# Weight sums of a seven-product block multiplication, formed in DRAM ahead of time instead of in SBUF on demand

## Chip, cores and metric

The kernel runs on one NeuronCore of a Trainium2 chip. The metric is the device time of one execution in microseconds, lower is better.

## The reference

A decoder trunk of two layers on a sequence of 512 tokens with 1024 features, float32. Layer 0 is a retention with four heads, layer 1 a stick-breaking attention with sixteen; each is followed by a gated feed-forward with a causal depthwise convolution of width 3. What the change touches is the last step of the feed-forward:

```python
def _conv_ffn(h, w_up, conv_w, conv_b, w_down):
    u = h @ w_up                       # 512 x 1024 @ 1024 x 5632
    u = lax.conv_general_dilated(...) + conv_b
    gate, val = jnp.split(u, 2, axis=-1)
    return (jax.nn.silu(gate) * val) @ w_down      # 512 x 2816 @ 2816 x 1024

for i in range(DEPTH):
    x = x + mixer_i(_rmsnorm(x, ...))  # retention, then stick-breaking
    x = x + _conv_ffn(_rmsnorm(x, ...), ...)
return _rmsnorm(x, final_norm)
```

## The kernel before

Activations lie in SBUF with features on the 128 partitions and tokens along the free dimension: eight tiles `x[m]` of 128x512. Every float32 product is made of three matmuls on a high and a low part in the type float32r (`mm3`, L133). Weights come from DRAM as chunks of 128x1024 (512 KB). `chunk` (L117) takes a `raw` buffer (`raw`, L114, three of them), loads it on SyncE's queue (L121), and `parts` (L124) casts it on ScalarE to `hi` (L129) and subtracts on VectorE to `lo` (L130); there are five buffers of `hi` and five of `lo`. A chunk feeds 24 matmuls of 512 columns in the projections. The source order gives a priority, and the framework fixes the order of instructions on each engine and queue when the kernel is built; each engine and each queue then works through its list in order and waits by semaphores.

`retention` (L371) reads x, makes the first four projections (`first4`, L144), forms the norm factor `self.r` by a `rsqrt` and then walks over four heads: `ret_qk`, `ret_v`, `ret_scores`, `ret_av`, `ret_y`, `out_proj`. `ret_v` uses four chunks together for 96 matmuls (`token_major`, L283).

`ffn` (L511) loops over the 22 blocks f of 128 hidden features: two up-projections, convolution, activation (`ffn_act`, L410). The down-projection goes in stages of blocks (`STAGES`). Layer 0 has stages of 8, 8 and 6 blocks, layer 1 of 8, 6 and 4, and then a tail of 4. The first two stages of each layer (`FAST`) are done by `fast_down` (L455), one call for each half of the output features, and start once the next two blocks are up-projected. Tokens are split in two halves, blocks in pairs, output features in quarters, and the 2x2 block product is made of seven products instead of eight. Each product multiplies a quarter-size weight, or a sum of such weights, by one of the operands that `ffn_act` prepared (`X11`, `T1`, `T2`, `T3`, `T4`, `X21`, `X22`). The weights are w11, w12, w21, w22 and the four sums

```
s1 = w21 + w22      s2 = s1 + w11      s3 = w11 + w21      s4 = s2 + w12
```

`quarter` (L445) issues the matmuls (L452) of one product for one of two PSUM banks; a product is 12 matmuls of 256 columns in each of two banks where the stage has 8 blocks, 9 where it has 6. After a product, `add` (L477) adds or subtracts the PSUM contents so far to the tiles `x[m]` on VectorE (L480). The products X11, T2, T3 and T4 accumulate in the banks `x`, T1 and X22 in `z`, X21 alone in two `acc` banks.

Before the change the sums are made in SBUF: a tile `sums` (two buffers) is loaded with w21 by SyncE (L471), w22 is added by a DMA that accumulates, issued by GpSimd (L469), the tile is split into hi and lo for T1, then w11 is accumulated onto it for T2, and later w12 for X22; a `raw` tile gets w11 and later w21 for T3. The products stand in the order T1, X11, T2, X21, T3, X22, T4.

Of the kernel before, what the change touches and what calls it, by code (L numbers as in the profile page):

```python
# [9 lines left out]
F32 = mybir.dt.float32  # L10
F32R = mybir.dt.float32r
AF = mybir.ActivationFunctionType
ALU = mybir.AluOpType
AX = mybir.AxisListType

P = 128
# [10 lines left out]
CH = 1024  # L27
STAGES = (((0, 8), (8, 16), (16, 22)), ((0, 8), (8, 14), (14, 18)))
FAST = (2, 2)
# [7 lines left out]
class Kernel:  # L37
# [12 lines left out]
    def __init__(self, ctx, tc, t):  # L50
        self.tc, self.nc, self.t = tc, tc.nc, t
        self.const = ctx.enter_context(tc.tile_pool(name="const", bufs=1))
        self.wp = ctx.enter_context(tc.tile_pool(name="wp", bufs=1))
        self.ap = ctx.enter_context(tc.tile_pool(name="ap", bufs=1))
        self.ps = ctx.enter_context(tc.tile_pool(name="ps", bufs=1, space=bass.MemoryType.PSUM))
        self.n = 0
        self.pp = None
        self.att_pool()
        self.phase("mix")
# [52 lines left out]
        return hi, lo  # L112

    def raw(self):  # L114
        return self.wp.tile([P, CH], F32, tag="raw", bufs=3, name=self.name("raw"))

    def chunk(self, c, cols=CH):  # L117

        nc = self.nc
        raw = self.raw()  # L120
        nc.sync.dma_start(raw[:, :cols], c)  # L121
        return self.parts(raw, cols)

    def parts(self, raw, cols=CH):  # L124
        nc = self.nc
        hi = self.wp.tile([P, CH], F32R, tag="hi", bufs=5, name=self.name("hi"))
        lo = self.wp.tile([P, CH], F32R, tag="lo", bufs=5, name=self.name("lo"))
        raw, hi, lo = raw[:, :cols], hi[:, :cols], lo[:, :cols]
        nc.scalar.copy(hi, raw)  # L129
        nc.vector.tensor_sub(lo, raw, hi.bitcast(F32))  # L130
        return hi, lo
# [101 lines left out]
    def setup(self):  # L233
        nc, t = self.nc, self.t
        c = lambda n, cols, dt=F32: self.const.tile([P, cols], dt, name=n)
        self.vec = c("vec", t["vec"].shape[1])
        nc.scalar.dma_start(self.vec[:, : 5 * KD], t["vec"][:, : 5 * KD])
        self.x = [c(f"x{m}", S) for m in range(KD)]
        self.ones = c("ones", P, F32R)
        nc.vector.memset(self.ones.bitcast(F32), 1.0)  # L240
        self.eps = c("eps", 1)
        nc.vector.memset(self.eps, EPS)

        nc.scalar.activation(c("table", 1), self.eps, AF.Sqrt)
        self.diag = c("diag", S)
        nc.vector.memset(self.diag, 0.0)

        warm = self.one()
        for i in range(WARM):
            nc.tensor.matmul(warm[:, :HALF], self.ones.bitcast(F32), self.diag[:, :HALF], start=i == 0, stop=i == WARM - 1)  # L250
        self.ident = self.diag[:, S - P :]
        nc.gpsimd.affine_select(
            out=self.ident, in_=self.ident, compare_op=ALU.not_equal, fill=1.0, base=0,
            pattern=[[-1, P]], channel_multiplier=1,
        )
# [115 lines left out]
    def retention(self):  # L371
        nc, t = self.nc, self.t
        first = self.first4("rfirst", load=True)
        self.cos, self.sin = self.sb("cs", S + P)[:, :S], self.sb("cs", S + P)[:, :S]
        nc.sync.dma_start(self.cos, t["cos"])
        nc.sync.dma_start(self.sin, t["sin"])
        nc.sync.dma_start(self.vec[:, 5 * KD :], t["vec"][:, 5 * KD :])
        nc.vector.tensor_mul(self.cos, self.cos, self.r)
        nc.vector.tensor_mul(self.sin, self.sin, self.r)
        self.rc = self.token_major_r()  # L380
        y = None
        for h in range(RH):
            q, k, tail = self.ret_qk(h, first if h == 0 else [])
            v = self.ret_v(h)
            if 0 < h < RH - 1:
                self.out_proj("rout", 4 * (h - 1), y, None)
            p = self.ret_scores(h, q, k, tail)
            o = self.ret_av(h, v, p)
            last, y = y, self.ret_y(h, o)
        self.out_proj("rout", 4 * (RH - 2), last, None)  # L390
        self.out_proj("rout", 4 * (RH - 1), y, 1)
# [63 lines left out]
    def fast_down(self, l, s, ops, half):  # L455


        nc, t = self.nc, self.t[f"fast{l}_{s}"][half]
        cols = 2 * len(ops) * P
        w11, w12, w21, w22 = t[0], t[1], t[2], t[3]  # L460
        first, second = slice(0, Q), slice(Q, S)
        x = [self.psum("x", 2) for _ in range(2)]
        z = [self.psum("z", 2) for _ in range(2)]
        sums = self.wp.tile([P, CH], F32, tag="sums", bufs=2, name=self.name("sums"))
        raw = self.raw()

        def load(to, w, add=False):
            if add:
                nc.gpsimd.dma_start(to[:, :cols], w, accum_op=ALU.add)  # L469
            else:  # L470
                nc.sync.dma_start(to[:, :cols], w)  # L471

        def product(to, w, n, start=False):
            for p in range(2):
                self.quarter(to[p], w, p, ops, n, start)

        def add(row, tokens, of, sign=1):  # L477
            for p in range(2):
                x = self.x[4 * half + 2 * p + row][:, tokens]
                (nc.vector.tensor_add if sign > 0 else nc.vector.tensor_sub)(x, x, of[p][:, :Q])  # L480

        load(sums, w21)
        load(sums, w22, True)
        load(raw, w11)
        w = self.parts(sums, cols)
        product(z, w, self.T1, True)
        add(1, second, z, -1)
        load(sums, w11, True)
        w = self.parts(raw, cols)
        product(x, w, self.X11, True)  # L490
        add(0, first, x)
        load(raw, w21, True)
        w = self.parts(sums, cols)
        product(x, w, self.T2)
        add(0, second, x)
        load(sums, w12, True)
        w = self.chunk(w12, cols)
        y = [self.acc() for _ in range(2)]
        product(y, w, self.X21, True)
        add(0, first, y)  # L500
        w = self.parts(raw, cols)
        product(x, w, self.T3)
        add(1, second, x, -1)
        w = self.parts(sums, cols)
        product(z, w, self.X22)
        add(0, second, z)
        w = self.chunk(w22, cols)
        product(x, w, self.T4)
        add(1, first, x, -1)

    def ffn(self, l, last):  # L511
        a, s = [], 0
        first = self.first4(f"ufirst{l}")
        self.phase("ffn")
        for f in range(NF):
            a.append(self.ffn_act(l, f, first[2 * f : 2 * f + 2] if f < 2 else (None, None)))
            if f == 1:
                self.swap_pool()
            if s < 2 and f == STAGES[l][s][1] + 1:
                lo, hi = STAGES[l][s]  # L520
                for half in range(2):
                    self.fast_down(l, s, a[lo + 1 : hi : 2], half)
                s += 1
        self.swap_pool()
        self.down(l, a, s, last)
        self.phase("mix" if last is not None else None)
        return a
# [310 lines left out]
```

## Time and profile before

| | |
|---|---|
| median of 3 runs | 1402.52 us (1402.23 to 1402.61) |
| the profiled execution | 1401.99 us, span 1400.2 us |
| TensorE busy | 1371.3 us, 98% of the span |
| VectorE busy | 1012.9 us, 72% |
| ScalarE busy | 618.4 us, 44% |
| mean granted TensorE clock | 0.994 |
| moved by DMA | 142.69 MB, 102 GB/s over the span |

The profile is of one execution. The span runs from its first to its last instruction; the execution's own time is 1.8 us longer. Engines are named PE (TensorE), PEld (its weight loads), DVE (VectorE), ACT (ScalarE), POOL (GpSimd) and SP (SyncE); a q behind the name is the engine's queue of DMA issues or its sequencer. L129 is line 129 of the kernel. Busy TensorE time is the union of its matmuls, whose records overlap, so the pace is read from the distance of their starts. A granted clock of 1.00 is 2.4 GHz, a lower mean says that part of the stretch ran at 1.2 GHz.

### The profile page before, as it was taken

What the parts mean: (1) busy time and instruction counts of PE and PEld (TensorE: products, weight loads), DVE (VectorE), ACT (ScalarE), POOL (GpSimd) and SP (SyncE); (2) the same over time, 40 slices, a digit from 0 to 9 for tenths busy, and PEclk for the clock granted to TensorE, in tenths of its full rate; (3) what the DMA queues carried; (4) which work ended last, traced back from release to release, by engine and by line L of the source; (5) the groups of instructions that cost most, each with busy time, mean ns of one, the idle gap of its engine ahead of it and who ended that gap; (6) DMA issues with size and microseconds to landing.
All of it is one profiled execution on the core that took longest, in us unless ns stands there. A gap on an engine that the chain in (4) does not pass through costs nothing.

```text
span 1400.2 us, 18420 instructions
## 1 busy us (share of the span) xinstructions
PE 1371.3 (98%) x7208; PEld 1163.2 (83%) x7208; DVE 1012.9 (72%) x1416; ACT 618.4 (44%) x876; POOL 34.8 (2%) x101
## 2 busy tenths in 40 slices
PE   9999999999999998999999999999999998998997
PEld 7888888888888888889888888787788897897887
DVE  7764564655669885777667788989799875776765
ACT  6433332434355442444344654654265443343434
POOL 0000000000000000001000000000000010010000
PEclk9999999999999999999999999999999999999999
DMA  8433133222233357336622422111133365245231
GB/s 288 122 94 103 55 107 104 62 90 73 78 91 120 105 108 184 103 96 135 177 77 65 134 84 62 61 54 39 45 108 119 95 127 170 84 87 162 62 89 61
DMA packets 45638, 142.69 MB, mean 102 GB/s; under 512 B 5104, under 2 KB 7280, under 8 KB 45552
## 3 DMA queue, kind: packets, MB, share of 16 engines
q1 hardware_dynamic: 39424, 124.45, 28.8%
q0 software_dynamic: 4608, 15.73, 6.8%
q10 hardware_dynamic: 1520, 1.33, 0.3%
q8 instruction: 57, 0.93, 0.3%
q14 instruction: 29, 0.24, 0.1%
HBM read 139.40 MB, written 2.10 MB: 101 GB/s over the span
## 4 chain that ended last, share of the span: by engine, by line
PE 84%; issue 7%; DVE 4%; DMA 3%; ACT 1%; POOL 0%; DVEq 0%; ACTq 0%; POOLq 0%
PE acc L136 21%; PE acc L138 21%; PE acc L137 21%; PE x L452 4%; PE att L136 3%; PE att L137 3%; PE att L138 3%; DMA sums<-in_fast 3%; PE z L452 2%; PE one L608 2%; PE z L582 1%; PE tp L600 1%; PE acc L452 1%; DVE lo L130 1%; ACT hi L129 1%
## 5 line engine op out<-in xcount | busy, mean ns | idle before, releaser
L129 ACT CAST hi<-raw 128x1024 fp32r<-128x1024 f32 (+2 forms) x253 | 244.3, 967 | 395.6 <-PE acc L137 257.9
L137 PE MATMUL acc<-xl,hi 128*128 128x512 f32 x960 | 374.6, 390 | 0.0
L136 PE MATMUL acc<-xh,hi 128*128 128x512 f32 x960 | 374.2, 390 | 0.0
L138 PE MATMUL acc<-xh,lo 128*128 128x512 f32 x960 | 374.2, 390 | 0.0
L130 DVE TENSOR_TENSOR lo<-raw,hi 128x1024 fp32r<-128x1024 f32 (+2 forms) x253 | 281.5, 1114 | 49.6 <-ACT hi L129 48.0
L138 PEld LDWEIGHTS acc<-xh,lo 128*128 128x128 f32 x960 | 180.2, 188 | 37.9 <-issue 0.5
L136 PEld LDWEIGHTS acc<-xh,hi 128*128 128x128 f32 x960 | 180.2, 188 | 36.9 <-issue 0.5
L137 PEld LDWEIGHTS acc<-xl,hi 128*128 128x128 f32 x960 | 180.3, 188 | 35.8
L404 DVE SCALAR_TENSOR_TENSOR tt<-tt,vec,tt 128x511 f32<-128x511 f32 (+1 forms) x176 | 131.1, 747 | 4.3 <-ACT tt L402 1.7
L401 DVE TENSOR_TENSOR tt<-acc,rr 128x512 f32<-128x512 f32 x80 | 55.1, 688 | 73.3 <-PE acc L138 73.3
L138 PE MATMUL acc<-hi,xl 128*128 128x512 f32 (+1 forms) x256 | 86.0, 336 | 0.0
L137 PE MATMUL acc<-lo,xh 128*128 128x512 f32 (+1 forms) x256 | 85.9, 336 | 0.0
L136 PE MATMUL acc<-hi,xh 128*128 128x512 f32 (+1 forms) x256 | 85.9, 336 | 0.0
L188 DVE TENSOR_TENSOR x<-x,acc 128x512 f32<-128x512 f32 x72 | 48.9, 685 | 50.6 <-PE acc L138 50.4
L452 PE MATMUL x<-oh,hi 128*128 128x256 f32 x240 | 70.4, 293 | 14.3 <-DVE x L480 14.3
L402 ACT ACTIVATE tt<-tt,vec 128x512 f32<-128x512 f32 x88 | 71.4, 812 | 10.1 <-DVE tt L401 9.0
L136 PE MATMUL acc<-yy,hi 128*128 128x512 f32 x192 | 75.1, 391 | 0.0
L138 PE MATMUL acc<-yy,lo 128*128 128x512 f32 x192 | 75.1, 391 | 0.0
L137 PE MATMUL acc<-yy,hi 128*128 128x512 f32 x192 | 75.0, 391 | 0.0
L452 PE MATMUL x<-ol,hi 128*128 128x256 f32 x240 | 69.8, 291 | 0.0
L452 PE MATMUL x<-oh,lo 128*128 128x256 f32 x240 | 69.7, 290 | 0.0
L452 PEld LDWEIGHTS x<-oh,hi 128*128 128x128 f32 x240 | 48.1, 200 | 15.0 <-ACT hi L129 9.7
(173 smaller groups left out, 2297.4 us busy)
## 6 DMA issues: line engine op xcount, KB each, us to landing
raw<-in_up SPq DMA_DIRECT2D x80, 512.0 KB, 3.7
sums<-in_fast POOLq DMA_DIRECT2D x18, 512.0 KB, 5.5
raw<-in_fast SPq DMA_DIRECT2D x18, 512.0 KB, 3.6
raw<-in_rv SPq DMA_DIRECT2D x16, 512.0 KB, 3.6
raw<-in_rg SPq DMA_DIRECT2D x16, 512.0 KB, 4.1
raw<-in_rout SPq DMA_DIRECT2D x16, 512.0 KB, 3.6
raw<-in_rqk SPq DMA_DIRECT2D x12, 512.0 KB, 3.6
raw<-in_sqk SPq DMA_DIRECT2D x12, 512.0 KB, 3.7
```

What stands on the lines that cost most here:

```text
L129: nc.scalar.copy(hi, raw)
L130: nc.vector.tensor_sub(lo, raw, hi.bitcast(F32))
L136: mm(out, a[0], b[0], start=start, stop=False)
L137: mm(out, a[0], b[1], start=False, stop=False)
L138: mm(out, a[1], b[0], start=False, stop=stop)
L188: self.nc.vector.tensor_add(self.x[m], self.x[m], ps)
L401: nc.vector.tensor_mul(u, ps, self.r)
L402: nc.scalar.activation(c, u, AF.Identity, scale=w[2], bias=w[3])
L404: nc.vector.scalar_tensor_tensor(c[:, i:], u[:, : S - i], w[2 - i], c[:, i:], op0=ALU.mult, op1=ALU.add)
L452: mm(out[:, :Q], a[ai], b[bi], start=start and k + i == 0, stop=k == nk - 1 and i == 2, skip_group_check=not start)
L582: nc.tensor.matmul(z[:, :nz], q[:, i * P : (i + 1) * P], k[:, :nz], start=m == 0, stop=m == 1)
L608: self.nc.tensor.matmul(o[e * DH : (e + 1) * DH, i * P : (i + 1) * P], v[p // 4 * NT + j][:, h * DH : (h + 1) * DH], aT[e][:, j * P : (j + ...
```

## The change

The four sums of each half of each fast stage are made once, in DRAM tiles, by transfers that GpSimd issues, during the retention (`weight_sums`, called after the first `rsqrt`, gated by a copy on GpSimd of one column of `self.r`). For each stage and half these are four plain copies and four accumulating transfers: w21 to s1, w11 to s3, then w22 onto s1, w21 onto s3; s1 to s2, w11 onto s2; s2 to s4, w12 onto s4. `fast_down` then loads each of its seven weights with `chunk`, as the projections do, in the order X11, T1, T2, X21, T3, X22, T4. The tiles `sums` are gone, and `raw` has five buffers instead of three. The matmuls, the adds to x and the arithmetic of a sum stay.

```diff
     def raw(self):
-        return self.wp.tile([P, CH], F32, tag="raw", bufs=3, name=self.name("raw"))
+        return self.wp.tile([P, CH], F32, tag="raw", bufs=5, name=self.name("raw"))
...
+        self.dp = ctx.enter_context(tc.tile_pool(name="dp", bufs=1, space=bass.MemoryType.DRAM))
...
+        self.gate = c("gate", 1)
...
         self.rc = self.token_major_r()
+        self.weight_sums()
...
-        w11, w12, w21, w22 = t[0], t[1], t[2], t[3]
+        w11, w12, w22 = t[0], t[1], t[3]
+        s1, s2, s3, s4 = (d[half] for d in self.sums[l, s])
...
-        sums = self.wp.tile([P, CH], F32, tag="sums", bufs=2, name=self.name("sums"))
-        raw = self.raw()
-
-        def load(to, w, add=False):
-            if add:
-                nc.gpsimd.dma_start(to[:, :cols], w, accum_op=ALU.add)
-            else:
-                nc.sync.dma_start(to[:, :cols], w)
...
         def product(to, w, n, start=False):
+            w = self.chunk(w, cols)
             for p in range(2):
                 self.quarter(to[p], w, p, ops, n, start)
...
-        load(sums, w21)
-        load(sums, w22, True)
-        load(raw, w11)
-        w = self.parts(sums, cols)
-        product(z, w, self.T1, True)
+        product(x, w11, self.X11, True)
+        add(0, first, x)
+        product(z, s1, self.T1, True)
         add(1, second, z, -1)
-        load(sums, w11, True)
-        w = self.parts(raw, cols)
-        product(x, w, self.X11, True)
-        add(0, first, x)
-        load(raw, w21, True)
-        w = self.parts(sums, cols)
-        product(x, w, self.T2)
+        product(x, s2, self.T2)
         add(0, second, x)
-        load(sums, w12, True)
-        w = self.chunk(w12, cols)
         y = [self.acc() for _ in range(2)]
-        product(y, w, self.X21, True)
+        product(y, w12, self.X21, True)
         add(0, first, y)
-        w = self.parts(raw, cols)
-        product(x, w, self.T3)
+        product(x, s3, self.T3)
         add(1, second, x, -1)
-        w = self.parts(sums, cols)
-        product(z, w, self.X22)
+        product(z, s4, self.X22)
         add(0, second, z)
-        w = self.chunk(w22, cols)
-        product(x, w, self.T4)
+        product(x, w22, self.T4)
         add(1, first, x, -1)
+
+    def weight_sums(self):
+        nc, tc, t = self.nc, self.tc, self.t
+        self.sums = {}
+        gate = nc.gpsimd.tensor_copy(self.gate, self.r[:, :1])
+        gate = getattr(gate, "ins", gate)
+        with tc.issue_after(gate):
+            for l in range(2):
+                for s in range(FAST[l]):
+                    cols = t[f"fast{l}_{s}"].shape[3]
+                    v = [[None] * 2 for _ in range(4)]
+                    for half in range(2):
+                        for i in range(4):
+                            d = self.dp.tile([P, cols + 16], F32, tag=f"s{l}{s}{i}{half}", bufs=1, name=self.name("sum"))
+                            v[i][half] = d[:, :cols]
+                    self.sums[l, s] = v
+                    for to, of, add in ((0, 2, 0), (2, 0, 0), (0, 3, 1), (2, 2, 1), (1, None, 0), (1, 0, 1), (3, None, 0), (3, 1, 1)):
+                        for half in range(2):
+                            w = t[f"fast{l}_{s}"][half][of] if of is not None else v[0 if to == 1 else 1][half]
+                            if add:
+                                nc.gpsimd.dma_start(v[to][half], w, accum_op=ALU.add)
+                            else:
+                                nc.gpsimd.dma_start(v[to][half], w)
```

## Rows read from the trace of the kernel before

**Rows 1.** The page, part 1: busy time, share of the span, instructions.

```profile
PE 1371.3 (98%) x7208; PEld 1163.2 (83%) x7208; DVE 1012.9 (72%) x1416; ACT 618.4 (44%) x876; POOL 34.8 (2%) x101
```

**Rows 2.** Stretches: us, busy PE, PEld, DVE, ACT, POOL; clock, DMA share, GB/s.

```profile
512.02:558.78 46.76, 42.05 (x338) 41.87 (x336) 32.01 (x49) 16.78 (x16) 4.36 (x5) 0.96 0.68 169
645.84:691.00 45.16, 42.22 (x338) 41.87 (x337) 29.76 (x46) 15.88 (x16) 4.43 (x6) 0.96 0.68 174
1130.60:1177.00 46.40, 41.77 (x338) 41.59 (x337) 32.10 (x49) 16.77 (x16) 4.36 (x5) 0.96 0.64 159
1242.30:1278.45 36.15, 31.96 (x253) 31.75 (x252) 25.82 (x45) 13.66 (x16) 2.62 (x3) 0.95 0.51 129
...
15.00:20.00 5.00, 5.00 (x23) 4.14 (x23) 4.47 (x8) 3.02 (x6) 0.00 (x0) 1.00 1.03 368
...
35.00:40.00 5.00, 5.00 (x24) 4.14 (x23) 5.00 (x9) 2.11 (x5) 1.53 (x2) 1.00 0.87 170
...
30.00:486.00 456.00, 455.50 (x2075) 379.19 (x2074) 296.78 (x388) 184.44 (x247) 1.88 (x2) 1.00 0.32 95
...
512.00:534.00 22.00, 22.00 (x185) 21.97 (x184) 17.14 (x27) 9.55 (x9) 2.62 (x3) 1.00 0.66 144
...
544.00:562.00 18.00, 18.00 (x131) 17.44 (x131) 10.11 (x16) 5.25 (x5) 0.86 (x1) 0.94 0.69 198
```

**Rows 3.** Timeline of TensorE: first matmul of the first stage, first after it.

```profile
512.02 0.28 PE L452 MATMUL z<-oh,hi 128*128 128x256 f32 x1
...
558.78 0.40 PE L136 MATMUL acc<-xh,hi 128*128 128x512 f32 x1
```

**Rows 4.** Chain of waits in the first fast stage (start, us, what).

```profile
534.33 5.60 DMA sums<-in_fast
540.03 1.05 ACT hi L129
...
542.80 4.61 PE x L452 x24
547.42 2.88 PE acc L452 x24
```

**Rows 5.** Waits of TensorE and the SP queue (total us, times, longest).

```profile
PE x L452 <- DVE x L480: 14.3, 4, 4.7
...
PE att L136 <- ACT pp L327: 0.4, 1, 0.4
...
SPq L121 <- DVE lo L130: 991.8, 206, 22.7
```

**Rows 6.** The page, parts 3 and 6: DMA queues, and issues to landing.

```profile
q1 hardware_dynamic: 39424, 124.45, 28.8%
q0 software_dynamic: 4608, 15.73, 6.8%
...
sums<-in_fast POOLq DMA_DIRECT2D x18, 512.0 KB, 5.5
raw<-in_fast SPq DMA_DIRECT2D x18, 512.0 KB, 3.6
```

**Rows 7.** Timeline of VectorE near the end of the first fast stage.

```profile
549.56 0.41 DVE L480 TENSOR_TENSOR x<-x,acc 128x256 f32<-128x256 f32 x1
...
551.29 1.23 DVE L130 TENSOR_TENSOR lo<-raw,hi 128x1024 fp32r<-128x1024 f32 x1 [0.54 <-ACT hi L129]
```

**Rows 8.** Landing times: loads before 30 us, and the tile sums.

```profile
raw<-in_rv SPq DMA_DIRECT2D x4, 512.0 KB, 5.4
...
DMA to landing us min/median/max: 2.7/5.4/8.5
```

**Rows 9.** The chain of waits in the first head.

```profile
48.76 3.91 DMA raw<-in_rqk
...
53.80 0.52 ACT pp L327
...
55.10 0.23 PE acc L136
```

## The prediction, made blind

> **What bounds the kernel now.** I read the page first: TensorE is busy 1371.3 of 1400.2 us [rows 1], so only 28.9 us of its idle time can be won, plus whatever it lost at a low clock. The busy share cannot say where these are, so the next view was the table by stretch, with one stretch for each of the four `fast_down` stages (two in each layer) [rows 2]; their ends are the first matmul of the stage and the first of another line after it [rows 3]. TensorE is idle there for 46.76 - 42.05 = 4.71, 2.94, 4.63 and 4.19 us, together 16.47. The granted clock of the same rows is 0.95 to 0.96, so part of each stage ran at 1.2 GHz instead of 2.4.
>
> The chain of waits shows the cause in the first stage [rows 4]. In its second half the chain goes through a transfer `sums<-in_fast` (5.60 us to landing) and the ScalarE cast of that tile, and only then do 24 matmuls start, which take 4.61 us where the next 24 take 2.88: the low clock comes behind the pause. TensorE's wait is listed as one on VectorE's add to x [rows 5]; by the chain the add only stood behind the late split of `sums` in VectorE's queue. The transfer is the accumulating one that makes w21+w22+w11 of w21+w22 in place: it can't start before the earlier product's split has read the tile, and the next product's weights can't be cast before it lands. Two `sums` buffers hide this in a first half (no idle time from 512 to 534 [rows 2]), not in a second.
>
> A matmul of 256 columns takes 2.88/24 = 0.12 us at full clock [rows 4]. A stage of 8 blocks has 14 products of 24, 40.32 us; the one of 6 blocks 14 of 18, 30.24 us. The stages take 46.76, 45.16, 46.40 and 36.15 us [rows 2]. The differences, 6.44, 4.84, 6.08 and 5.91, sum to **23.27 us**: 16.47 idle and 6.80 of slow clock. The other idle time, 28.9 - 16.47 = 12.4 us, lies outside these stages and is not touched.
>
> **The change, part by part.**
>
> *Removed: the accumulating transfers on the path.* After it every product's weights are a plain chunk: load, cast, subtract, as in the up-projection. No chunk depends on another, so loads and casts run ahead as far as five raw and five hi/lo buffers allow. A plain 512 KB load of `in_fast` lands in 3.6 us against 5.5 for an accumulating one [rows 6]. Whether chunks can feed a product every 2.88 us I read from the end of the first stage, where the remaining products of before were already cast ahead or plain: the 24 matmuls from 547.42 on take their 2.88 us [rows 4]. There VectorE needs 1.23 us for a subtraction and 0.41 for each of two adds, 2.05 us a product [rows 7], and ScalarE 1.05 [rows 4], both under 2.88. Over a whole stage VectorE's 32.01 us (25.82 in the last) stand against 40.32 (30.24) [rows 2]. Loads: 512 KB each 2.88 us is 182 GB/s; 198 GB/s moved between 544 and 562 with a DMA share of 0.69 [rows 2], accumulating transfers included. So I take the whole 23.27 us as won; the lower bound is 16.47 less a restart at low clock, should a small pause remain.
>
> *Moved: the order of the products.* X11 now comes first and T1 second. X11, then T2 into the same `x` banks becomes X11, T1, T2, which puts 2.88 us between the product and its successor in the bank. In exchange the last product of the first half (T4, into x) is followed directly by X11 of the second half. One bank has 1.44 us from its own end to its next matmul, as the other bank's 12 matmuls lie between. In the steady stretch the add of the first bank (at 549.56, done 549.97) ended 0.33 us before the other bank's matmuls did, at 547.42 + 2.88 = 550.30 [rows 4, 7]. So 0 as the value; if a subtraction of 1.23 us stands one place worse, 1.23 - 0.33 = 0.9 us at each of four boundaries, 3.6 us as the upper bound. I put 0.4 us.
>
> *Moved and added: 64 transfers on GpSimd's queue after the first `rsqrt`.* Each half of a stage makes four plain copies and four accumulates, all with a DRAM destination: 32 + 32 transfers of 512 KB (384 KB in the last stage), 15.73 MB plain and 15.73 MB accumulating. GpSimd's queue is blocked while they wait for each other; what is behind them in that queue are the small memsets of the attention, which follows the first feed-forward. Engine time: the queue of accumulating transfers used 6.8% of 1400.2 us for 15.73 MB, 6.05 us for each MB, and the plain queue 28.8% for 124.45 MB, 3.24 us [rows 6]. That gives 51 + 95 = 146 us if DRAM to DRAM costs what DRAM to SBUF does; I know no row for a DRAM destination, so doubled, 292 us, is the other end. The stretch from 30 to 486 has a share of 0.32, or 146 us [rows 2]; it would rise to 0.64, or 0.96 at the high end. Below one either way, and the sums of layer 0's first stage, a quarter of it, are wanted only shortly before 512 us [rows 3].
>
> What the loads feel: between 15 and 20 us the share was 1.03 and TensorE stayed busy [rows 2]; loads then landed in 5.4 us instead of 3.6 [rows 8]. The sensitive place is the burst of casts after `ret_v`, where four chunks come free together: there ScalarE waits for `raw<-in_rqk` (3.91 us) in front of the cast `pp` that TensorE needs [rows 9], and TensorE lost 0.4 us [rows 5]. If such a load took the 8.5 us that the slowest transfer of `sums` took [rows 8], about 5 us at each of four heads, 20 us, would be the upper bound. Against it stand five raw buffers instead of three: four loads may be complete before the burst, and the queue of loads waited mostly for a buffer (991.8 us on `lo`) [rows 5], not for data. The lower bound is -0.5, all idle time of TensorE between 30 and 486 [rows 2]. I take +1.5 us, nearer to the low end, as the only such wait in the trace cost 0.4.
>
> The Trainium skill (DMA: Bandwidth & Descriptors, Issuing engines are not separate DMA queues) says that transfers from GpSimd and SyncE share the same 16 engines and interleave, so moving work to GpSimd's queue frees no bandwidth. The trace agrees as far as it goes: with two accumulates in flight between 35 and 40 us the share was 0.87 at only 170 GB/s [rows 2]. By the rule alone the retention pays for the sums, which is rival 3 below; by the share of 0.32 there is room for them, and the sum keeps its +1.5.
>
> *Also moved:* 24 more plain loads (11.8 MB, 38 us of the engines) enter the fast stages, where 95 us of accumulating transfers leave: cover enough. The `gate` copy of one column costs GpSimd a fraction of a microsecond, beside nothing.
>
> **The sum.** Against the profiled execution: 1401.99 - 23.27 + 0.4 + 1.5 = 1380.6; its median neighbours are 0.53 higher (1402.52), so **1381.1 us**, 1.5% faster. Measurement tells apart about 0.2%, 2.8 us.
>
> **The rivals.**
> 1. *Contention takes back a good part.* Loads in the retention land at 6 to 9 us, ScalarE stands in front of late casts, and TensorE pays some microseconds per head: 5 to 15 us, so 1384 to 1395. For it: rows 9's chain runs through a load already; against it: the two extra buffers. Chance 0.13.
> 2. *A pause stays in the fast stages.* The first half also carries VectorE's leftover activation work: 17.14 of 22 us between 512 and 534 [rows 2]. If adds and subtractions queue wrongly at the half boundary, one pause per stage with its slow restart stays: half of 23.27 kept, 1402.5 - 11.6 + 1.5 = 1392. Against it: no pause in the first halves of before with the same VectorE work. Chance 0.08.
> 3. *Slower: the loads starve while the sums are made.* Place: 30 to some 330 us, the high engine time of above. Retention takes 95 GB/s [rows 2]. If transfers to DRAM hold each DMA engine so long that the loads get less, TensorE runs at the loads' rate. Buffers filled ahead (five chunks of 24 matmuls at 0.23 us [rows 9], 5.5 us each) cover 27 us. To lose 23.27 + 2.8 over 300 us, (300 x (1 - r/95)) - 27 = 26, r must fall to 78 GB/s. With two queues taking turns at 3.24 and 6.05 us per MB the loads get 1/(9.29 us per MB) = 108 GB/s; with 12 us, 66 GB/s, a loss of 65 us, near 1445. It also needs GpSimd's queue to be always full, while each step waits for the one before it. Chance 0.10.
> 4. *Nothing measurable*, gains and costs cancelling within 2.8 us: 0.05.
>
> **How the numbers follow.** My forecast, 1377 to 1384, has 0.64; rivals 1 and 2 are faster too, so faster 0.85, same 0.05, slower 0.10. The range from 1377 to 1394 leaves out 0.15 above and little below: below 1378.7 only other waits could pay.
>
> **What would show it.** Each fast stage at about 40.3 us (30.2 for the last) from its first to its last matmul, no wait on the add beyond a microsecond, clock 1.00 there; no accumulating transfer after the retention; a DMA share near 0.6 in the part of the retention where the sums are made, and TensorE busy without a gap there. The prediction is wrong if TensorE's idle time appears between 30 and 486 us behind `raw` loads, or if a pause with a clock below 1 remains at the boundary of two halves.

## The result, and the profile after

The changed kernel takes 1377.81 us (median of 4 runs, 1377.61 to 1378.58), the one before 1402.57 us in the same session (4 runs). The ratio is 0.9822, 95% interval 0.9805 to 0.9839: 1.8% faster, where 1.5% was forecast (1381.1 us). The profiled execution took 1378.58 us with a span of 1376.8, against 1401.99 and 1400.2 before: 23.4 us less, close to what the prediction had summed over the fast stages (23.27).

The first view again is the table by stretch, with one stretch for each fast stage, from its first matmul to the first of another line behind it; then three stretches of the retention. The columns are those of [rows 2].

```profile
511.27:551.67 40.40, 40.40 (x337) 40.35 (x336) 32.34 (x49) 16.98 (x16) 0.00 (x0) 1.00 0.54 170
638.74:679.10 40.36, 40.36 (x337) 40.36 (x336) 30.13 (x46) 15.99 (x16) 0.10 (x1) 1.00 0.56 169
1119.00:1159.41 40.41, 40.41 (x338) 40.36 (x336) 32.34 (x49) 16.99 (x16) 0.00 (x0) 1.00 0.55 170
1224.72:1255.05 30.33, 30.33 (x254) 30.28 (x252) 26.23 (x45) 13.84 (x16) 0.00 (x0) 1.00 0.64 193
...
0.00:30.00 30.00, 28.40 (x113) 22.96 (x114) 22.96 (x32) 21.41 (x33) 0.49 (x5) 1.00 0.91 325
30.00:200.00 170.00, 170.00 (x784) 141.90 (x783) 109.05 (x147) 64.97 (x92) 44.73 (x65) 1.00 1.00 276
200.00:511.27 311.27, 311.27 (x1407) 258.82 (x1406) 207.87 (x265) 130.64 (x169) 0.00 (x0) 1.00 0.29 90
```

The stages take 40.40, 40.36, 40.41 and 30.33 us instead of 46.76, 45.16, 46.40 and 36.15 [rows 2], TensorE is busy for the whole of each, and the granted clock is 1.00. Together that is 151.50 instead of 174.47: **22.97 us**. From 30 us to the first stage TensorE has no idle time left, where it had 0.50, and the first stage starts 0.75 us earlier; the stretches between and behind the stages take 0.3 us more in all: 22.97 + 0.75 - 0.3 = 23.4. The reader should see the price of this in the sixth row: from 30 to 200 us the DMA engines are busy without a break (share 1.00) at 276 GB/s, and TensorE does not notice.

Next, the page's part 1 and the DMA queues (part 3), the whole list of TensorE's waits, and the first and the last DMA issue for the sums on GpSimd's queue.

```profile
PE 1364.9 (99%) x7208; PEld 1157.4 (84%) x7208; DVE 1014.2 (74%) x1416; ACT 618.8 (45%) x876; POOL 51.4 (4%) x134
...
q1 hardware_dynamic: 42880, 136.25, 30.9%
q0 software_dynamic: 8704, 31.46, 9.3%
```

```profile
PE one L252 <- DVE diag L248: 1.6, 1, 1.6
PE tp L609 <- DVE pp L601: 0.9, 2, 0.5
PE one L617 <- DVE pp L610: 0.3, 1, 0.3
```

```profile
32.03 2.24 POOL L518 DMA_DIRECT2D sum<-in_fast  x4
...
191.95 1.76 POOL L516 DMA_DIRECT2D sum<-in_fast  x2 [3.15 <-DMA sum<-sum]
```

The wait on the add to x, 14.3 us in [rows 5], is gone, and none has taken its place: what is left lies in the start and in the attention. TensorE's busy time fell too, by 6.4 us (1371.3 to 1364.9), with the same 7208 matmuls: that is what the matmuls behind the pauses had taken longer at 1.2 GHz. The last two transfers are issued at 192 us, so all sums are ready at about 200, some 311 us before the first stage begins. All 31.46 MB took 9.3% of the engines' span, 128 us.

### The profile page after: what moved, and what is told of

The parts are those of the page before. It is cut to its first block, busy times and chain, and to the rows that moved or that the text cites. A ratio compares the mean times of both kernels' runs of the same rounds, so it can differ in the third digit from the quotient of the medians.

```text
span 1376.8 us, 18478 instructions
## 1 busy us (share of the span) xinstructions
PE 1364.9 (99%) x7208; PEld 1157.4 (84%) x7208; DVE 1014.2 (74%) x1416; ACT 618.8 (45%) x876; POOL 51.4 (4%) x134
## 3 DMA queue, kind: packets, MB, share of 16 engines
q0 software_dynamic: 8704, 31.46, 9.3%
## 4 chain that ended last, share of the span: by engine, by line
PE 96%; DVE 3%; issue 0%; ACT 0%; DVEq 0%
PE acc L139 23%; PE acc L137 23%; PE acc L138 23%; PE x L455 6%; PE att L137 4%; PE att L138 4%; PE att L139 4%; PE z L455 3%; PE acc L455 2%; PE one L617 2%; PE z L591 1%; PE tp L609 1%; DVE cs L597 1%; DVE lo L131 0%; DVE tt L563 0%; DVE tt L560 0%
## 5 line engine op out<-in xcount | busy, mean ns | idle before, releaser
L130 ACT CAST hi<-raw 128x1024 fp32r<-128x1024 f32 (+2 forms) x277 | 268.3, 969 | 432.4 <-PE acc L138 274.5
L131 DVE TENSOR_TENSOR lo<-raw,hi 128x1024 fp32r<-128x1024 f32 (+2 forms) x277 | 309.4, 1118 | 55.4 <-ACT hi L130 53.7
L597 DVE TENSOR_TENSOR_SCAN cs<-pp,diag 128x512 f32<-128x512 f32 (+3 forms) x64 | 52.1, 819 | 3.3 <-ACT pp L593 2.2
```

The lines of the kernel that those rows point to most:

```text
L597: nc.vector.tensor_tensor_scan(left[:, :n][:, ::-1], sg[:, :n][:, ::-1], self.diag[:, S - n :][:, ::-1], 0.0, op0=ALU.mult, op1=ALU.max,)
```

## The experiments

The theory: the accumulating transfers between one product and the next were the whole loss; anything that takes them off the path wins some 23 us, and what they cost in the retention is hidden as long as loads are issued early enough. The rivals: the wait was for the add, so the order of the products won it; the two additional buffers won it; or contention costs something, only postponed or not seen. Eleven kernels were run, each with a ratio to the kernel before on the same chip. As the chip's session moves both, ratios are compared, or the time of kernels of one session.

**1. The old order of products in the changed kernel.**

```diff
-        product(x, w11, self.X11, True)
-        add(0, first, x)
         product(z, s1, self.T1, True)
         add(1, second, z, -1)
+        product(x, w11, self.X11, True)
+        add(0, first, x)
```

> The changed kernel with the products in the old order T1, X11, T2, so that T2 follows X11 in the same PSUM banks again. My theory: the order is worth nothing by itself, stages within 0.5 us of 40.4 and 30.3, 1377 to 1380 us. Rival (TensorE's wait was for VectorE's add, as its list of waits says, and the new order removed it): pauses on the add come back in the second halves, 4 to 14 us, 1382 to 1392 us.

Measured: 1378.17 us, ratio 0.9808 [0.9794, 0.9823]. The stages of the profiled execution:

```profile
510.44:550.80 40.36, 40.36 (x337) 40.36 (x336) 32.36 (x49) 16.97 (x16) 0.00 (x0) 1.00 0.55 170
637.87:678.22 40.35, 40.35 (x338) 40.35 (x337) 30.12 (x46) 16.00 (x16) 0.10 (x1) 1.00 0.56 170
1118.11:1158.47 40.36, 40.36 (x337) 40.36 (x336) 32.35 (x49) 16.97 (x16) 0.00 (x0) 1.00 0.55 170
1223.78:1254.14 30.36, 30.36 (x254) 30.31 (x253) 26.22 (x45) 13.84 (x16) 0.00 (x0) 1.00 0.65 191
```

They agree with those of the changed kernel to 0.05 us. T2 directly behind X11 in the same banks costs nothing, nor does X11 behind T4 at the boundary of two halves: a bank's add fits under the other bank's matmuls either way. With the chain of [rows 4] and experiment 2, the wait on the add in [rows 5] was a name, not a cause.

**2. The new order alone, in the kernel before.** The sums stay in SBUF, three raw buffers.

```diff
         load(sums, w21)
         load(sums, w22, True)
         load(raw, w11)
-        w = self.parts(sums, cols)
-        product(z, w, self.T1, True)
-        add(1, second, z, -1)
-        load(sums, w11, True)
         w = self.parts(raw, cols)
         product(x, w, self.X11, True)
         add(0, first, x)
+        w = self.parts(sums, cols)
+        product(z, w, self.T1, True)
+        add(1, second, z, -1)
+        load(sums, w11, True)
         load(raw, w21, True)
```

> The kernel before with the new order of the products alone; sums in SBUF as before, three raw buffers. My theory (the chain of accumulating transfers is the cause): T1 and T2 become neighbours, so the transfer between them has no product of 2.88 us beside it any more: pauses in the second halves grow by up to 2.9 us per stage, some perhaps in first halves too: 1402 to 1420 us, not faster. Rival (the order carries the gain, through the add to x): 1380 to 1392 us.

Measured: 1405.16 us, ratio 0.9994 [0.9984, 1.0005]: the time can't be told from the kernel before. The first two stages, and the wait of TensorE in the list of waits:

```profile
511.96:559.98 48.02, 42.20 (x337) 41.99 (x336) 31.36 (x49) 17.21 (x17) 4.35 (x5) 0.93 0.64 161
647.05:695.04 47.99, 41.92 (x338) 41.74 (x337) 30.66 (x48) 16.12 (x17) 4.45 (x6) 0.93 0.67 170
```

```profile
PE x L452 <- DVE x L480: 20.7, 5, 6.1
```

The pauses stay. In this one execution, the slowest of its ten, the four stages take 178.8 us instead of 174.5 and the listed wait is 20.7 us instead of 14.3, as expected with T1 and T2 next to each other; by the time over all runs that growth is not shown, only that the order wins nothing.

**3. Three raw buffers in the changed kernel.**

```diff
-        return self.wp.tile([P, CH], F32, tag="raw", bufs=5, name=self.name("raw"))
+        return self.wp.tile([P, CH], F32, tag="raw", bufs=3, name=self.name("raw"))
```

> The changed kernel with three raw buffers instead of five. My theory (the accumulating transfers on the path were the loss; contention in the retention is hidden by loads issued early): the four fast stages stay at 40.4, 40.4, 40.4 and 30.3 us, and TensorE loses up to 5 us between 30 and 200 us, where loads land in some 6 us and only three can be under way: 1378 to 1383 us. Rival A (the two extra buffers hid the contention and carry a good part of the gain): 10 us or more of idle time between 30 and 200 us, 1388 us or more. Rival B (buffers do nothing here): 1377.5 to 1378.5 us.

Measured: 1387.64 us, ratio 0.9876 [0.9861, 0.9890]. Some 9.5 us are lost again (experiments 1 and 7 took 1378.17 and 1378.49 in the same session), more than I had allowed. The fast stages did not lose them: with three buffers they take 40.42, 40.37, 40.42 and 30.34 us, so the two extra buffers have no part in the gain there. The first and the last:

```profile
521.05:561.47 40.42, 40.42 (x338) 40.37 (x337) 32.32 (x49) 16.97 (x16) 0.00 (x0) 1.00 0.56 170
1234.20:1264.54 30.34, 30.34 (x254) 30.28 (x252) 26.04 (x45) 13.85 (x16) 0.00 (x0) 1.00 0.62 182
```

Rival A was nearly right in size, for a reason that the timelines show. First SyncE's queue in this kernel (two rows, then a load in the chain of waits) and ScalarE about the burst of casts in the first head, then both in the changed kernel. A row of the queue gives the start of its first issue and the time from there to the end of its last.

```profile
32.52 15.01 SPq L122 DMA_DIRECT2D raw<-in_rg  x2
48.97 12.38 SPq L122 DMA_DIRECT2D raw<-in_rqk  x4
...
48.97 9.65 DMA raw<-in_rqk
```

```profile
56.23 1.04 ACT L130 CAST hi<-raw 128x1024 fp32r<-128x1024 f32 x1 [7.40 <-DMA raw<-in_rg]
57.18 0.68 ACT L304 ACTIVATE vv<-acc,rc 128x512 f32<-128x512 f32 x1
58.69 1.04 ACT L130 CAST hi<-raw 128x1024 fp32r<-128x1024 f32 x1 [0.83 <-DMA raw<-in_rqk]
59.65 1.03 ACT L329 CAST pp<-tt 128x512 fp32r<-128x512 f32 x2
```

```profile
18.46 6.89 SPq L122 DMA_DIRECT2D raw<-in_rg  x4
27.74 4.67 SPq L122 DMA_DIRECT2D raw<-in_rqk  x2
```

```profile
51.16 1.04 ACT L130 CAST hi<-raw 128x1024 fp32r<-128x1024 f32 x1
52.66 0.62 ACT L329 CAST pp<-tt 128x512 fp32r<-128x512 f32 x1 [0.46 <-DVE tt L327]
```

With three buffers the last load of `rg` and the first of `rqk` are issued only inside the burst, at 47 to 49 us, when a buffer comes free. Beside the sums' transfers the `rqk` load takes 9.65 us (3.91 in [rows 9]). ScalarE stands 7.40 us in front of the cast of `rg` and 0.83 us in front of that of `rqk`, whose data are late, and the cast `pp` that TensorE wants next is behind them, at 59.65 instead of 52.66. TensorE's list has one long wait more, and the stretches show the slow clock behind it:

```profile
PE att L137 <- ACT pp L329: 6.3, 1, 6.3
```

```profile
30.00:60.00 30.00, 24.00 (x113) 20.06 (x111) 22.61 (x35) 11.00 (x18) 9.01 (x13) 0.97 0.97 289
60.00:100.00 40.00, 39.69 (x175) 33.02 (x176) 25.60 (x34) 16.07 (x23) 10.01 (x15) 0.93 1.02 282
```

With five buffers six chunks are issued from 18 to 32 us, ahead of the sums, and the burst finds its data there. In the kernel before, the same chain had cost 0.4 us [rows 5, 9].

**4. Four raw buffers** (the same line, `bufs=4`).

> The changed kernel with four raw buffers. With three, two loads were issued at 47 to 49 us, in the burst itself, and landed 9.7 us later; with four one of them is issued earlier. My theory (the price is that of loads that are issued only in the burst and stand in a queue behind each other): most of the 10 us goes, 1378 to 1382 us. Rival (in proportion to the buffers): about 1383 us.

Measured: 1377.61 us, ratio 0.9809 [0.9794, 0.9823], all of it back. With one buffer more the four loads of `rg` are issued from 22 to 28 us and the first of `rqk` at 32; the fifth buffer shows no gain.

**5. Three raw buffers, no transfers for the sums.** `fast_down` loads single quarters instead of the sums, so their additions are left out.

```diff
-        self.weight_sums()
...
-        s1, s2, s3, s4 = (d[half] for d in self.sums[l, s])
+        s1, s2, s3, s4 = t[2], t[0], t[2], t[1]
```

> Three raw buffers and no transfers for the sums (single quarters are loaded in place of the sums, so the output differs and only the time is read). With three buffers and the sums' transfers the kernel had taken 1387.6 us, one pause of 6.3 us behind a late load at 58 us. My theory now: the two extra buffers are worth something only beside the sums' transfers, so 1377.5 to 1379.5 us here. Rival (three buffers are too few by themselves for seven plain loads in each half): 1384 us or more.

Measured: 1378.99 us, ratio 0.9818 [0.9801, 0.9834]. Without the sums three buffers cost 1.4 us at most (1378.99 beside 1377.61 for experiment 4 in the same session; the intervals of the two ratios overlap), with them some 9.5 us: it is the two together. The profiled execution, at 1381.56 us the slowest of its four, has the same wait of TensorE for `pp`, of 1.8 us.

**6. Three raw buffers, the sums gated later**, on the output of the first head.

```diff
-        self.weight_sums()
...
             o = self.ret_av(h, v, p)
+            if h == 0:
+                self.weight_sums(o[0][:, :1])
...
-    def weight_sums(self):
+    def weight_sums(self, when):
...
-        gate = nc.gpsimd.tensor_copy(self.gate, self.r[:, :1])
+        gate = nc.gpsimd.tensor_copy(self.gate, when)
```

> Three raw buffers, and the sums gated on the output of the first head (some 65 us) instead of the first norm factor, so that the first head's burst of casts lies ahead of them and two later bursts lie beside them. In the kernel with three buffers the second head's burst, beside the sums too, had cost about 0.5 us. My theory (the first head alone is exposed, as its loads are the first ones and nothing is ahead): 1378 to 1381 us. Rival (any burst beside the sums costs what the first did): 1387 us or more.

Measured: 1380.43 us, ratio 0.9832 [0.9817, 0.9846]. By the ratios (0.9876 to 0.9832) some 6 of the 9.5 us come back by moving the transfers past the first head's burst; 2.8 us are left to experiment 4 in the same session. Two later bursts lie beside the sums now, and the only new wait of TensorE above half a microsecond is 1.6 us for an add to x, behind a late load of `rg`. So the first head is the exposed one. ScalarE in the second head shows why:

```profile
134.22 1.05 ACT L130 CAST hi<-raw 128x1024 fp32r<-128x1024 f32 x1 [6.07 <-DMA raw<-in_rg]
138.07 1.05 ACT L130 CAST hi<-raw 128x1024 fp32r<-128x1024 f32 x1 [2.79 <-DMA raw<-in_rg]
...
153.86 1.34 ACT L329 CAST pp<-tt 128x512 fp32r<-128x512 f32 x3 [1.89 <-DVE tt L327]
```

Its loads are as late as those of the first head, and ScalarE waits 6.07 us for one. But in the second and third heads `out_proj` stands between `ret_v` and `ret_scores`, so TensorE has other matmuls from 127 us on and wants `pp` only at 154, when the late casts are done; in the first head nothing stands between.

**7. No transfers for the sums, five raw buffers** (the edit of 5 in the changed kernel; the additions are left out).

> The changed kernel without the 64 transfers on GpSimd's queue; the sums are left out, single quarters of the weights are loaded in their place, so the output differs and only the time is read. It prices the contention: my theory, by the trace after (no idle time of TensorE between 30 and 486 us), says 0, so 1377 to 1379 us. Rival (the saturated engines between 30 and 200 us cost time that does not show as idle time): 1 to 3 us faster than the changed kernel, 1375 to 1376.5 us.

Measured: 1378.49 us, ratio 0.9810 [0.9796, 0.9825], beside 1378.17 for experiment 1 in the same session. Taking the transfers away wins nothing that the measurement can tell: with five buffers their price is zero within it.

**8. Every step of the sums twice.**

```diff
-                    for to, of, add in ((0, 2, 0), ...
+                    for to, of, add in 2 * ((0, 2, 0), ...
```

> The changed kernel with every step of the sums made twice (copy again, accumulate again), which doubles the traffic to about 63 MB and the time with saturated engines from 170 to some 340 us. It tells a free steady state from a price that the buffers filled ahead only postponed. My theory: loads get at least the 95 GB/s that the retention takes, so nothing is lost: 1377 to 1379 us. Rival (the loads got less, say 80 GB/s, and the chunks filled ahead, some 27 to 55 us of work, paid for it in 170 us): over 340 us the store runs empty, 10 to 30 us slower, 1388 to 1408 us.

Measured: 1378.26 us, ratio 0.9811 [0.9797, 0.9826].

```profile
30.00:200.00 170.00, 170.00 (x784) 141.89 (x783) 109.11 (x147) 65.13 (x92) 44.27 (x66) 1.00 1.00 283
200.00:370.00 170.00, 170.00 (x784) 141.83 (x784) 97.00 (x124) 62.91 (x85) 44.31 (x64) 1.00 0.95 257
```

For 340 us the engines are nearly saturated (shares 1.00 and 0.95) and TensorE is never idle. Nothing was paid out of a store: the queue of loads moved 15.01 MB in the first of the two stretches and 13.73 MB in the second (88 and 81 GB/s), as without any transfers for the sums (15.21 and 13.38 MB in experiment 7).

**9. Three quarters of the sums made during the first fast stage**, where TensorE takes a chunk each 2.88 us.

```diff
-        self.weight_sums()
+        self.sums = {}
+        self.weight_sums(self.r[:, :1], ((0, 0),))
...
                 lo, hi = STAGES[l][s]
+                if (l, s) == (0, 0):
+                    self.weight_sums(a[hi - 1][0].bitcast(F32)[:, :1], ((0, 1), (1, 0), (1, 1)))
...
-    def weight_sums(self):
+    def weight_sums(self, when, which):
...
-        gate = nc.gpsimd.tensor_copy(self.gate, self.r[:, :1])
+        gate = nc.gpsimd.tensor_copy(self.gate, when)
...
-            for l in range(2):
-                for s in range(FAST[l]):
+            if True:
+                for l, s in which:
```

> The changed kernel with the sums of the first stage made as before in the retention, those of the other three stages gated on the last operand of the first stage, so that they are made from the start of the first fast stage on. There TensorE takes a 512 KB chunk each 2.88 us, 182 GB/s, and the sums want as much again. My theory: with half of the 280 GB/s for each, loads get 140 GB/s; 14 chunks less five filled ahead take up to 9 us longer, so the first stage grows from 40.4 to 42 to 50 us and the total to 1379 to 1388 us; the up-projections behind it, at 103 GB/s, lose nothing. Rival (the retention's zero price holds here too): stage at 40.4 us, 1377 to 1379 us.

Measured: 1378.04 us, ratio 0.9809 [0.9792, 0.9825]. My expectation of a longer stage was wrong. The stage, and the two queues from 505 to 552 us (packets, MB, share), with the queue of loads in the changed kernel over the same time as the last row:

```profile
510.99:551.40 40.41, 40.41 (x337) 40.36 (x336) 32.34 (x49) 17.00 (x16) 8.55 (x14) 1.00 1.04 335
```

```profile
q0 software_dynamic: 2156, 7.85, 62.9%
q1 hardware_dynamic: 2016, 7.36, 39.5%
...
q1 hardware_dynamic: 2086, 7.57, 50.4%
```

The loads moved 7.36 MB in 47 us, 157 GB/s, where they move 7.57 MB, 161 GB/s, with nothing beside them. So they got nearly all that was asked, and the stage never asked for its 182 GB/s at once: in both kernels eight of its 14 chunks are issued before 505 us, the last at 526, 25 us before the stage ends. The step that my expectation had wrong is that only five chunks are filled ahead. What loads would get if 182 GB/s were asked beside the sums, this run does not show.

**10. No gate: the sums from the very start.**

```diff
+        self.weight_sums()
         first = self.first4("rfirst", load=True)
...
         self.rc = self.token_major_r()
-        self.weight_sums()
...
-        gate = nc.gpsimd.tensor_copy(self.gate, self.r[:, :1])
-        gate = getattr(gate, "ins", gate)
-        with tc.issue_after(gate):
+        if True:
```

> The changed kernel with the sums' transfers issued at the very start, without the gate on the first norm factor. At the start TensorE takes 512 KB (a weight chunk and a tile of x) each 12 matmuls of 0.23 us, 2.7 us, 190 GB/s. My theory (contention is free only while TensorE takes less than the engines leave): the 4.2 MB of the first eight steps at about half of the 280 GB/s that saturated engines moved take 30 us instead of 22, so 5 to 10 us of idle time before 40 us: 1383 to 1388 us. Rival (loads are served first wherever the transfers are): 1377 to 1379 us.

Measured: 1407.77 us, ratio 1.0022 [1.0011, 1.0033]: 0.2% slower than the kernel before, the whole gain and a little more is gone. The direction was right, the size (30 us, not 5 to 10) was not. Stretches, then queues and landing times before 30 us; in the changed kernel the loads `rfirst` and `xT` landed in 5.0 and 5.3 us.

```profile
0.00:30.00 30.00, 22.40 (x69) 15.18 (x69) 11.25 (x19) 12.43 (x20) 8.64 (x18) 0.94 0.98 306
30.00:60.00 30.00, 19.36 (x71) 14.87 (x71) 14.02 (x15) 10.19 (x14) 7.39 (x11) 0.77 1.05 337
60.00:100.00 40.00, 36.33 (x170) 30.09 (x169) 30.49 (x46) 16.31 (x27) 9.28 (x15) 0.96 1.03 303
```

```profile
q0 software_dynamic: 1537, 5.64, 64.2%
q1 hardware_dynamic: 1924, 3.52, 33.6%
...
raw<-in_rfirst SPq DMA_DIRECT2D x8, 256.0 KB, 14.3
x<-in_xT SPq DMA_DIRECT2D x8, 256.0 KB, 15.7
raw<-in_rv SPq DMA_DIRECT2D x1, 512.0 KB, 15.1
```

The loads moved 3.52 MB in 30 us, 117 GB/s, where I had put the need at 190; in the changed kernel they move 9.70 MB there, 323 GB/s. TensorE is idle 7.60 + 10.64 + 3.67 = 21.9 us up to 100 us, 20.3 more than in the changed kernel; with the span 29.8 us longer, the other 9.5 us go with the low clock of these stretches (0.94, 0.77, 0.96). I had priced the first eight steps alone. SyncE's queue is one list, so the loads behind them (the first of `rv` took 15.1 us) were late too.

**11. Eight blocks in the second fast stage of layer 1.**

```diff
-STAGES = (((0, 8), (8, 16), (16, 22)), ((0, 8), (8, 14), (14, 18)))
+STAGES = (((0, 8), (8, 16), (16, 22)), ((0, 8), (8, 16), (16, 18)))
```

> The changed kernel with the second fast stage of layer 1 made of eight blocks instead of six (stages 0 to 8, 8 to 16, 16 to 18), as a seven-product stage no longer costs a pause. One pair more by seven products: 14 x 6 matmuls of 0.12 us, 10.08 us, instead of 8 x 2 x 3 of 0.228, 10.94 us: 0.9 us faster if VectorE's additional operand work is hidden, 1376.5 to 1378 us. Rival: the chunks of the last stage, only 256 columns for six matmuls, come too slowly behind the fast stage, 1379 us or more.

Measured: 1377.23 us, ratio 0.9805 [0.9790, 0.9819], beside 1378.04 and 1378.26 for experiments 9 and 8 in the same session. The 0.9 us would fit, but it is below what the measurement tells apart; the interval holds the ratios of those two (0.9809 and 0.9811).

## Why the prediction came out right

- *The loss in the fast stages*, 23.27 us: measured 22.97. Experiments 1 and 2 separate the accumulating transfers from the order: sums as plain chunks with either order take 40.4 and 30.3 us a stage, sums accumulated in SBUF pause with either order. Experiment 3 takes the buffers out of it. What in the transfers mattered more, their length (5.5 us against 3.6 [rows 6]) or that each works in place on a tile that the product before must have split first, was not separated, nor was a kernel run with more `sums` tiles.
- *The order of products*, put at +0.4 us with 3.6 as bound: 0 by experiment 1.
- *Contention*, put at +1.5 us: 0 with five buffers (experiments 7 and 8), and some 9.5 us with three (experiment 3). The place was the one named, the burst of casts in the first head with `raw<-in_rqk` in front of `pp` (and a load of `rg` before it); so was what stands against it, the additional buffers. The bound of 5 us at each of four heads had the wrong shape: one head paid nearly all, 6.3 us idle and most of the rest in slow clock, and in the next two `out_proj` covers the late loads (experiment 6).
- *The DMA share*, forecast near 0.6 while the sums are made: wrong, it was 1.00 for 170 us. The engine time was smaller than either end (128 us, not 146 to 292), and 0.64 came from spreading it over 456 us; the transfers ran as fast as the engines took them, in 170 us. No step of the sum hung on it except rival 3, which experiment 8 rejects for the retention and experiment 10 shows at the start, where loads move 323 GB/s when left alone and nothing is loaded ahead. The rule of the Trainium skill that the prediction weighed (DMA: Bandwidth & Descriptors, Issuing engines are not separate DMA queues) says that transfers of all issuing engines run on the same 16 DMA engines and interleave. The trace agrees: beside the sums' transfers a load of 512 KB landed in 5.9 to 9.2 us instead of 3.6 to 4.3 (medians by tensor, 30 to 200 us). That the retention pays for the sums did not follow from it: the place decided whether the sharing cost time.
- *The sum.* Of the 3.3 us between 1381.1 and 1377.81, 1.9 are the two terms that were not paid, and 0.1 is left of smaller differences of the profiled executions (0.75 us gained ahead of the first stage, 0.3 less than forecast in the stages, 0.3 lost between them). The other 1.3 us are chance: the profiled execution was 0.53 us below the median before the change and is 0.77 above it after. So 1377.81 lies below the 1378.7 under which "only other waits could pay", and near the low end of the range, without another wait having paid more than a fraction of a microsecond.

The two parts of the change that win nothing alone are not alike: the order can be left out, a fourth buffer can't. Two `sums` tiles and three `raw` buffers take as much of SBUF as five `raw` buffers, each tile being 128x1024; five buffers beside the `sums` tiles were not tried.

## What to carry to other kernels

A value that only depends on weights can be made far ahead of its use in time that the DMA engines have free, and the consumer then has no chain of transfers between its steps; look for the stretch where compute takes much less than the engines can move, and keep the transfers away from the start, where nothing is loaded ahead. Saturated DMA engines did no harm here to loads issued early: the exposed place was a load issued when it is needed, whose consumer stands in an in-order queue ahead of urgent work, and one more buffer was the cure. A wait put down to the last of several producers can be a name only; following the chain back shows what was late, and undoing each part by itself confirms it.

## What the runs showed of the hardware

- DRAM-to-DRAM copies and accumulates together took 128 us of the 16 engines for 31.46 MB, 4.1 us per MB, less than the 6.05 of the accumulates into SBUF [rows 6].
- Beside the sums' transfers the loads moved what was asked where they could be issued ahead: 90 GB/s from 30 to 200 us with the transfers and 89 without them (experiment 7), 157 from 505 to 552 us (experiment 9) and 161 without. At the start they moved 117 GB/s (experiment 10) where they move 323 alone. With 512 KB transfers under way on the other queue a load of 512 KB landed in 5.9 to 9.2 us (medians by tensor, 30 to 200 us in the changed kernel) instead of 3.6 to 4.3 before, without a loss where it had been issued early.
- A pause of TensorE of 6.3 us was followed by a granted clock of 0.93 over the next 40 us.
